# Four plain first groups, an earlier count of ready tiles and an earlier split in a hybrid decoder layer

## The chip, the cores and the metric

The kernel runs on one core of a Trainium2 chip. The metric is the time of one execution on the device in microseconds (us), the median of several runs. Its five engines are named as the profile names them: TensorE is PE (its weight loads PEld), VectorE is DVE, ScalarE is ACT, GpSimd is POOL and SyncE is SP. SP issues nearly all DMAs.

## What is computed

One decoder layer on 256 tokens with a model width of 2048, all in float32, cut to its core:

```python
mod = silu(c) @ w_ada + b_ada
shift1, scale1, gate1, shift2, scale2, gate2 = split(mod, 6)
h = rms_norm(x, g_norm1) * (1 + scale1) + shift1
p = h @ w_in            # 2048 x 12288: retention q,k,v,g | HGRN2 q,f,i,g | gates A, B
y_a = (head_layer_norm(retention(rope(q), rope(k), v)) * silu(g)) @ w_ret_o
y_b = (head_rms_norm(hgrn2(silu(q), f, i)) * silu(g)) @ w_hg_o
x = x + gate1 * ((sigmoid(ga) * y_a + sigmoid(gb) * y_b) @ w_out)
h2 = rms_norm(x, g_norm2) * (1 + scale2) + shift2
a, b = split(causal_conv3(h2 @ w_up))      # 2 x 5632 columns
x = x + gate2 * ((silu(a) * b) @ w_down)
out = rms_norm(x, g_final)
```

Both heads work on chunks of 128 tokens.

## The kernel before

**Products in three parts.** A float32 product is made of three products of a shorter format (fp32r). Weights come by DMA into a buffer `raw` (`load`, L161, at most 11 at a time). ACT copies them into a high part `wh` (`upper`, L176), DVE makes the rest `wl = raw - wh` (`rest`, L181); there are four buffers of each. The activations `hT` have a high and a low part too. A product is high x high, low x high and high x low: L205, L206 and L210 where tokens or columns lie in rows (`mm_rows`), L221, L222 and L225 in the other form (`mm_cols`). `mm_plain` (L231) multiplies the unsplit weights by an unsplit activation as plain float32; its matmuls appear twice each in the profile. `mm_apart` (L242) does the three parts of several groups in turn.

**Pieces and visits.** The first stage makes 12 groups of 512 columns of `w_in` (`ATT`, numbered 0 to 11). The contraction has 16 k tiles of 128. A group can't be done in one go, because the activation tile k exists only after the conditioning for it: `ada1(k)` multiplies 2 MB of `w_ada` by silu(c) on DVE (`ada_dot`, four times L507 for a tile, each with its own `raw`), puts scale and shift together on ACT (L518, L519, L524) and makes the tile on ACT and DVE (`modulated`, L434, L435, L436). So a table of **visits** `(group, m, work)` goes round the groups, and each visit adds m new k tiles to its group; `work` counts units, one k tile of one group. `READY` says at which `work` one more k tile counts as ready. A visit works in **pieces** of two k tiles, or of one where m is odd, each with its own load, split and matmuls. It takes a PSUM bank pair `pg` (there are two), and at its end `take` evicts it: ACT copies it the first time (L880), DVE adds it to the accumulator later (L882). Groups 0 and 1 keep their banks `po` throughout (`RESIDENT = 2`).

Ahead of the table stands a start written by hand for the first four groups (`FIRST = 4`) and k tiles 0 and 1: groups 0 and 1 take tile 0 as plain products, groups 2 and 3 take it as split ones, and then all take tile 1. In this part `pin` keeps instructions in the order of the program; behind it (`self.ordered = False`) the recording layer puts them in an order of its own, so that what the code traces first need not come first on an engine.

**What runs beside it.** `pump`, once for each piece, advances background work by a credit: the conditioning tiles, then the two halves of the HGRN2 head (`hgrn`), retention and the later conditioning vectors. `finish(*ada[:have])` forces the tiles that a visit needs. `early` traces the first piece of the next visit, its load and split, ahead of the present visit's eviction. `hgrn` for a half starts as soon as its three groups are done (0, 2, 4, then 1, 3, 5) and starts on ACT with a sigmoid (L617), which loads a function table; then come Sqrt (L629), Ln (L631) and exponentials, and at its end the head output: matmuls L763 and L765, squares on ACT (L769), a root (L353, with a table load of its own), and products on DVE (L773).

**The wide groups.** Behind the visits four groups of 512 columns are made by `wide_group` (L255 and L258). Each takes both `pg` pairs at once, one for each pair of output blocks, and goes through the k tiles in four steps of four tiles, in each step first one pair and then the other. At its end ACT copies a part (L276) and DVE adds the rest (L277), and only then is the pair free for the next group. The eight gate groups, `w_hg_o`, `w_ret_o`, `w_out`, `w_up` and `w_down` follow.

The two lines on which the table of visits rested:

```python
READY = (14, 24, 34, *range(45, 156, 11))
have = 2 + sum(work >= at for at in READY)
```

Of the kernel before, what the change touches and what calls it, by code (L numbers as in the profile page):

```python
# [12 lines left out]
F32 = mybir.dt.float32  # L13
# [3 lines left out]
AF = mybir.ActivationFunctionType  # L17
ALU = mybir.AluOpType
# [5 lines left out]
KT = D // P  # L24
# [5 lines left out]
G = 512  # L30
NORM_EPS = 1e-6
HEAD_EPS = 1e-5
FIRST = 4
RESIDENT = 2
ADA_EVERY = 11
READY = (14, 24, 34, *range(45, 156, 11))
NOSYNC = mybir.DependencyInfo(mybir.DependencyClass.NoSync, mybir.DependencyReason.DATA)
SMALL = 70
COLS = (8, 8)
# [21 lines left out]
class Kernel:  # L61
# [784 lines left out]
    def run(self):  # L846
        nc, a = self.nc, self.a
# [11 lines left out]
        def act(k):  # L859
            return hT[k // 2][:, k % 2, :]  # L860
# [13 lines left out]
        mms = [self.mm_rows if c0 in ROWS else self.mm_cols for c0 in ATT]  # L874

        def take(g, ps, fresh):
            for at, z in self.parts(ps, ATT[g] in ROWS):
                dst = accs[g][:, at, :]
                if fresh:
                    nc.scalar.activation(dst, z, AF.Copy)  # L880
                else:
                    nc.vector.tensor_tensor(dst, dst, z, ALU.add)  # L882
# [6 lines left out]
        def first(k):  # L889

            return self.scale_shift("ada1", k, s1, t1, self.gn1, fine=True)

        def opening(k):

            z = self.s1([P, T], name="z")
            self.pin(nc.scalar.activation(z, self.xT[0][:, k, :], AF.Identity, bias=self.dots[:, 0:1], scale=s1[:, k : k + 1]))
            return z

        ada = [None, None, *(ada1(k) for k in range(2, KT))]
        gen = first(0)  # L900
# [7 lines left out]
        z = opening(0)  # L908
        for _ in gen:
            pass  # L910
        h = self.s1([P, T], name="h")
        summed(h, z, self.dots)

        ps = {0: self.po2(), 1: self.po2()}
        hT[0] = self.blk([P, 2, 2 * T], F32R, name="hT")
        hi, lo = act(0)[:, :T], act(0)[:, T:]
        plain = [self.load(a["wa"][g][:, 0:1, :], 1, G) for g in range(RESIDENT)]
        uppers = []
        for g in range(RESIDENT, FIRST):
            if g == RESIDENT:  # L920
                self.pin(nc.scalar.activation(hi, h, AF.Copy))
            uppers.append(self.upper(a["wa"][g][:, 0:1, :], 1, G, shift=COLS))
        self.pin(nc.vector.tensor_tensor(lo, h, hi.bitcast(F32), ALU.subtract))
        rests = [self.rest(z) for z in uppers]
        self.times(1, 1, rx_sb)
        gen = first(1)
        for g in range(RESIDENT):
            self.mm_plain(ps[g], plain[g][:, 0, :], h)
        for g in range(RESIDENT, FIRST):
            ps[g] = self.pg()  # L930
            wh, wl = rests[g - RESIDENT]
            mms[g](ps[g], [(act(0), wh[:, 0, :], wl[:, 0, :])], True, False)
            for _ in range(2):
                next(gen)
        z = opening(1)
        for _ in gen:
            pass
        uppers = [self.upper(a["wa"][g][:, 1:2, :], 1, G, shift=COLS) for g in range(RESIDENT)]
        hi, lo = act(1)[:, :T], act(1)[:, T:]
        summed(hi, z, self.dots)  # L940
        h = self.s1([P, T], name="h")
        summed(h, z, self.dots)
        self.pin(nc.vector.tensor_tensor(lo, h, hi.bitcast(F32), ALU.subtract))
        rests = [self.rest(z) for z in uppers]
        self.mm_apart([ps[g] for g in range(RESIDENT)], rests, act(1))
        for g in range(RESIDENT, FIRST):
            wh, wl = self.rest(self.upper(a["wa"][g][:, 1:2, :], 1, G, shift=COLS))
            mms[g](ps[g], [(act(1), wh[:, 0, :], wl[:, 0, :])], False, True)
        begun = list(self.pieces(a["wa"][FIRST][:, 0:2, :], 2))
# [13 lines left out]
        def visit(g):  # L963
            return COLS if g in cols else (0, 0)
# [3 lines left out]
        def begin(kind, hb, *ins):  # L968
            att.append(self.start(kind(hb, *ins, gates)))

        def visits():
            work, g = sum(done), FIRST
            seen = list(done)
            while min(seen) < KT:
                have = 2 + sum(work >= at for at in READY)
                m = have - seen[g]
                if m > 0:
                    yield g, m, work
                    seen[g] = have
                    work += m  # L980
                else:
                    work += 0.5
                g = (g + 1) % len(ATT)
                if have == KT and seen[0] < KT:
                    g = min(i for i in range(len(ATT)) if seen[i] < KT)

        def early(g, m):
            k = done[g]
            pieces = self.pieces(a["wa"][g][:, k : k + m, :], m, shift=visit(g), raw=stock.pop(g, None))
            return chain([next(pieces)], pieces)  # L990

        small = False
        plan = list(visits())
        for g in range(RESIDENT, FIRST):
            take(g, ps[g], True)
        for n, (g, m, work) in enumerate(plan):
            if work > SMALL and not small:
                small = True
                self.small_loads(nc.sync, ("freq", "lbT", "lmask"))
                self.start(self.trig())  # L1000
                self.start(self.lower_bound())
            fresh = done[g] == 0
            have = done[g] + m
            self.finish(*ada[:have])
            bank = ps[g] if g < RESIDENT else self.pg()
            whole = g >= RESIDENT
            self.products(mms[g], bank, a["wa"][g], act, done[g], m, first=whole, last=whole or have == KT, shift=visit(g), begun=begun)
            done[g] = have
            begun = early(*plan[n + 1][:2]) if n + 1 < len(plan) else None
            if whole or have == KT:  # L1010
                take(g, bank, fresh or not whole)
            if have == KT and ATT[g] in GATES:
                nc.scalar.activation(accs[g], accs[g], AF.Silu)
                gates[GATES.index(ATT[g])] = accs[g]
            for hb in range(2):
                gs = [hb, 2 + hb, 4 + hb]
                if g in gs and min(done[i] for i in gs) == KT:
                    self.pace(0, 14.0, 24)
                    begin(self.hgrn, hb, *(accs[i] for i in gs))
                    for i in gs:  # L1020
                        accs[i] = None
# [63 lines left out]
        for j in range(4):  # L1085
            last = j == 3
            x1.append(self.load_rows(j))
            if not last:
                g = self.row(self.gate["gate1"], j, "g1")
            if j == 2:  # L1090
                g3 = self.row(self.gate["gate1"], 3, "g1")
            elif last:
                g = g3
            ps = self.products(self.mm_rows, self.po2() if last else self.pg(), a["wout"][j], actm, 0, KT, hold=4 * last, gain=g if last else None)
            if last:
                g = None
# [14 lines left out]
        begun = [next(up), next(up)]  # L1111
        pu = self.pg()[:2] + self.pg()[:2]

        def half(j, t):

            return self.modulated_half(turned[j], 2 * j, self.sc2, self.sh2, t)
# [6 lines left out]
        for t in range(NT):  # L1123
            self.residual(x1[3], ps, g, None, 3, t)
            if t == 1:
                h = half(0, 0)
# [272 lines left out]
```

## Time and profile before

| | |
|---|---|
| median of 3 runs | 1512.08 us (1510.61 to 1512.22) |
| the profiled execution | 1513.45 us |
| its span | 1511.7 us |
| PE, DVE, ACT busy | 1489.2, 1209.0, 836.8 us |
| HBM read | 382.11 MB, 254 GB/s over the span |

The span reaches from the first to the last instruction of the program that the profiler saw; the execution's own time has some 1.75 us around it. The profile is of one execution. In its rows a time is counted from the start of the span; a row of the timeline has start, duration, engine, line, operation, what is written and read, and in brackets the idle time of the engine before it with what ended it. The page's forty slices show where DMA is full: the first quarter and a bit.

```profile
DMA  9999997788688879989947777777777767667561
```

The first stage with its visits fills the time to about 293 us, the wide groups that to about 398 us.

### The profile page before, as it was taken

What the parts mean: (1) busy time and instruction counts of PE and PEld (TensorE: products, weight loads), DVE (VectorE), ACT (ScalarE), POOL (GpSimd) and SP (SyncE); (2) the same over time, 40 slices, a digit from 0 to 9 for tenths busy, and PEclk for the clock granted to TensorE, in tenths of its full rate; (3) what the DMA queues carried; (4) which work ended last, traced back from release to release, by engine and by line L of the source; (5) the groups of instructions that cost most, each with busy time, mean ns of one, the idle gap of its engine ahead of it and who ended that gap; (6) DMA issues with size and microseconds to landing.
All of it is one profiled execution on the core that took longest, in us unless ns stands there. A gap on an engine that the chain in (4) does not pass through costs nothing.

```text
span 1511.7 us, 22801 instructions
## 1 busy us (share of the span) xinstructions
PE 1489.2 (99%) x8537; PEld 1278.6 (85%) x8537; DVE 1209.0 (80%) x1651; ACT 836.8 (55%) x1207; POOL 4.0 (0%) x8
## 2 busy tenths in 40 slices
PE   9999999998999999999999999999999999999997
PEld 8788898887878888888888888888888888888886
DVE  7799997899899977888877787778777769455694
ACT  5655555866775664445456555555555558344342
POOL 0000000000000000000000000000000000000000
PEclk9999999999999999999999999999999999999999
DMA  9999997788688879989947777777777767667561
GB/s 372 329 337 333 333 332 259 233 287 280 216 268 295 295 259 333 318 292 344 338 133 233 245 228 242 238 233 234 233 243 230 228 195 201 197 206 213 179 188 56
DMA packets 111311, 385.73 MB, mean 255 GB/s; under 512 B 12848, under 2 KB 13408, under 8 KB 111200
## 3 DMA queue, kind: packets, MB, share of 16 engines
q1 hardware_dynamic: 110304, 383.14, 76.8%
q8 instruction: 67, 1.10, 0.3%
q10 hardware_dynamic: 896, 1.13, 0.2%
q14 instruction: 44, 0.36, 0.1%
HBM read 382.11 MB, written 2.11 MB: 254 GB/s over the span
## 4 chain that ended last, share of the span: by engine, by line
PE 93%; DVE 3%; ACT 1%; DMA 1%; issue 1%; DVEq 0%; ACTq 0%
PE pg L205 13%; PE pg L210 13%; PE pg L206 13%; PE po L1232 11%; PE pg L1232 10%; PE po L1234 5%; PE pg L1234 5%; PE pg L255 4%; PE po L210 3%; PE po L205 3%; PE po L206 3%; PE pg L258 2%; DVE raw L507 1%; DVE wl L181 1%; DMA raw<-in_wa 1%
## 5 line engine op out<-in xcount | busy, mean ns | idle before, releaser
L181 DVE TENSOR_TENSOR wl<-raw,wh 128x1024 fp32r<-128x1024 f32 (+1 forms) x534 | 633.5, 1194 | 229.5 <-ACT wh L176 215.1
L176 ACT ACTIVATE wh<-raw 128x1024 fp32r<-128x1024 f32 (+1 forms) x534 | 546.1, 1034 | 471.0 <-PE pg L206 192.2
L507 DVE SCALAR_TENSOR_TENSOR raw<-raw,sc 128x1024 f32<-128x1024 f32 (+2 forms) x194 | 234.4, 1212 | 0.0
L205 PE MATMUL pg<-wh,hT 128*128 128x512 f32 x512 | 203.3, 397 | 4.3 <-ACT wh L176 3.0
L206 PE MATMUL pg<-wh,hT 128*128 128x512 f32 x512 | 200.1, 391 | 0.0
L1232 PE MATMUL po<-h2T,wh 128*128 128x512 f32 x704 | 175.8, 392 | 0.0
L1232 PE MATMUL pg<-h2T,wh 128*128 128x512 f32 x688 | 172.2, 393 | 0.0
L1232 PEld LDWEIGHTS po<-h2T,wh 128*128 128x128 f32 x704 | 125.8, 188 | 21.6
L1232 PEld LDWEIGHTS pg<-h2T,wh 128*128 128x128 f32 x688 | 123.0, 188 | 21.1
L210 PE MATMUL pg<-wl,hT 128*128 128x512 f32 x512 | 139.3, 392 | 0.0
L205 PEld LDWEIGHTS pg<-wh,hT 128*128 128x128 f32 x512 | 96.5, 188 | 25.7 <-ACT wh L176 3.7
L210 PEld LDWEIGHTS pg<-wl,hT 128*128 128x128 f32 x512 | 96.7, 189 | 20.5
L206 PEld LDWEIGHTS pg<-wh,hT 128*128 128x128 f32 x512 | 96.5, 189 | 19.3
L1234 PEld LDWEIGHTS po<-h2T,wl 128*128 128x128 f32 x704 | 93.4, 188 | 7.5
L1234 PEld LDWEIGHTS pg<-h2T,wl 128*128 128x128 f32 x688 | 91.4, 188 | 7.3
L1234 PE MATMUL po<-h2T,wl 128*128 128x256 f32 x704 | 94.6, 277 | 0.0
L1234 PE MATMUL pg<-h2T,wl 128*128 128x256 f32 x688 | 92.5, 277 | 0.0
L255 PE MATMUL pg<-hT,wh 128*128 128x512 f32 x256 | 66.0, 401 | 4.7 <-DVE p L277 4.7
L206 PE MATMUL pg<-wh,gs 128*128 128x512 f32 x176 | 68.6, 390 | 0.0
L205 PE MATMUL pg<-wh,gs 128*128 128x512 f32 x176 | 68.6, 390 | 0.0
L205 PE MATMUL po<-wh,gs 128*128 128x512 f32 x176 | 68.6, 390 | 0.0
L206 PE MATMUL po<-wh,gs 128*128 128x512 f32 x176 | 68.5, 389 | 0.0
(271 smaller groups left out, 2021.1 us busy)
## 6 DMA issues: line engine op xcount, KB each, us to landing
raw<-in_wup SPq DMA_DIRECT2D x176, 512.0 KB, 4.6
raw<-in_wdown SPq DMA_DIRECT2D x88, 512.0 KB, 4.1
raw<-in_wa SPq DMA_DIRECT2D x80, 512.0 KB, 5.4
raw<-in_ada SPq DMA_DIRECT2D x64, 512.0 KB, 5.5
raw<-in_wab SPq DMA_DIRECT2D x64, 512.0 KB, 5.4
raw<-in_ada SPq DMA_DIRECT2D x62, 512.5 KB, 5.6
raw<-in_gate SPq DMA_DIRECT2D x32, 512.5 KB, 5.2
raw<-in_wk SPq DMA_DIRECT2D x32, 512.0 KB, 4.6
```

The source lines that it names most:

```text
L176: self.pin(self.nc.scalar.activation(wh, raw, AF.Copy))
L181: self.last = self.nc.vector.tensor_tensor(wl, raw, wh.bitcast(F32), ALU.subtract)
L205: nc.tensor.matmul(ps[t], lhsT=act[:, hi], rhs=wh, start=first and i == 0, stop=False)
L206: nc.tensor.matmul(ps[t], lhsT=act[:, lo], rhs=wh, start=False, stop=False)
L210: nc.tensor.matmul(ps[t], lhsT=act[:, hi], rhs=wl, start=False, stop=last and i == len(items) - 1)
L255: nc.tensor.matmul(ps[z], lhsT=wh[:, z * P : (z + 1) * P], rhs=act, start=first and i == 0, stop=False)
L258: nc.tensor.matmul(ps[z][:, :T], lhsT=wl[:, z * P : (z + 1) * P], rhs=act[:, :T], start=False, stop=last and i == len(items) - 1)
L507: dot = self.pin(nc.vector.scalar_tensor_tensor(raw[:, 0, :], raw[:, 0, :], 1.0, self.sc[:, at:to], ALU.mult, ALU.mult, accum_out=part[:, ...
L1232: self.pin(nc.tensor.matmul(ps[z], lhsT=wh[:, z * P : (z + 1) * P], rhs=act, start=kt == 0, stop=False, skip_group_check=bool(begun)))
L1234: nc.tensor.matmul(ps[z][:, :T], lhsT=wl[:, z * P : (z + 1) * P], rhs=act[:, :T], start=False, stop=kt == KT - 1, skip_group_check=bool(be ...
```

## The change

The diff, whole but for its context:

```diff
-READY = (14, 24, 34, *range(45, 156, 11))
+LAG = 1
...
-        plain = [self.load(a["wa"][g][:, 0:1, :], 1, G) for g in range(RESIDENT)]
-        uppers = []
-        for g in range(RESIDENT, FIRST):
-            if g == RESIDENT:
-                self.pin(nc.scalar.activation(hi, h, AF.Copy))
-            uppers.append(self.upper(a["wa"][g][:, 0:1, :], 1, G, shift=COLS))
-        self.pin(nc.vector.tensor_tensor(lo, h, hi.bitcast(F32), ALU.subtract))
-        rests = [self.rest(z) for z in uppers]
+        plain = [self.load(a["wa"][g][:, 0:1, :], 1, G) for g in range(FIRST)]
         self.times(1, 1, rx_sb)
         gen = first(1)
-        for g in range(RESIDENT):
+        for g in range(FIRST):
+            if g >= RESIDENT:
+                ps[g] = self.pg()
             self.mm_plain(ps[g], plain[g][:, 0, :], h)
-        for g in range(RESIDENT, FIRST):
-            ps[g] = self.pg()
-            wh, wl = rests[g - RESIDENT]
-            mms[g](ps[g], [(act(0), wh[:, 0, :], wl[:, 0, :])], True, False)
-            for _ in range(2):
+            if g == 1:
+                self.pin(nc.scalar.activation(hi, h, AF.Copy))
                 next(gen)
+                next(gen)
+                self.pin(nc.vector.tensor_tensor(lo, h, hi.bitcast(F32), ALU.subtract))
+        next(gen)
+        next(gen)
...
-                have = 2 + sum(work >= at for at in READY)
+                have = min(KT, 2 + int((work - LAG) / ADA_EVERY))
...
         plan = list(visits())
+        z = [n for n, (g, _, _) in enumerate(plan) if g == FIRST + 2]
+        for n, m in zip(z, (-1, 1)):
+            plan[n] = (plan[n][0], plan[n][1] + m, plan[n][2])
...
+            ahead = early(*plan[n + 1][:2]) if m <= 2 and n + 1 < len(plan) else None
             self.products(mms[g], bank, a["wa"][g], act, done[g], m, first=whole, last=whole or have == KT, shift=visit(g), begun=begun)
             done[g] = have
-            begun = early(*plan[n + 1][:2]) if n + 1 < len(plan) else None
+            begun = ahead or (early(*plan[n + 1][:2]) if n + 1 < len(plan) else None)
```

It has four parts. All four first groups take k tile 0 as plain products, so the two splits of weights for it go, and the low part of the activation is made later. The table of ready tiles becomes a formula: tile 3 counts as ready at 23 units rather than 24, and the visits fall otherwise on the groups. Group 6 takes one tile less in its first visit and one more in its second. And the next visit's first piece is traced ahead of the products wherever the present visit has at most two tiles. The table has 53 visits instead of 54; its last ones were (group, tiles) (3,3) (4,3) (5,2) (6,2) (7,1) (8,1) (9,1) (11,5) and are (3,3) (4,2) (5,2) (6,1) (7,1) (8,1) (10,5) (11,4). Tile 3 is first wanted in visit 10 (the tenth from 0, group 10, second piece) instead of visit 11; tiles 4 and 5 one unit sooner than before; tiles 6 to 15 after as many units as before.

How this moves instructions is shown at three places. The first is the start, on DVE, from the scale and shift of tile 0 (L887 writes `h`) to the dots for tile 1 (L507). Before:

```order
L887 TENSOR_SCALAR h_224<-z_216,dot_39_210 128x256
L923 TENSOR_TENSOR hT_230<-h_224,hT_230 128x256
L181 TENSOR_TENSOR wl_239<-raw_236,wh_238 128x512
L181 TENSOR_TENSOR wl_244<-raw_241,wh_243 128x512
L497 TENSOR_TENSOR xT_113<-xT_113,rx_sb 128x256
L507 SCALAR_TENSOR_TENSOR raw_272,dot_57_271<-raw_272,sc 128x1024
L507 SCALAR_TENSOR_TENSOR raw_275,dot_57_271<-raw_275,sc 128x1025
```

And of the changed kernel:

```order
L887 TENSOR_SCALAR h_224<-z_216,dot_39_210 128x256
L497 TENSOR_TENSOR xT_113<-xT_113,rx_sb 128x256
L507 SCALAR_TENSOR_TENSOR raw_250,dot_54_249<-raw_250,sc 128x1024
L507 SCALAR_TENSOR_TENSOR raw_253,dot_54_249<-raw_253,sc 128x1025
L928 TENSOR_TENSOR hT_230<-h_224,hT_230 128x256
L507 SCALAR_TENSOR_TENSOR raw_270,dot_59_269<-raw_270,sc 128x1024
```

The two `wl` are gone, and the low part (L923, now L928) stands behind two dots.

The second place is the end of the visits, on DVE: the adds of groups 5 to 8 (`p_174` to `p_177`) among the splits of the next pieces. Before, with the scans of the HGRN2 head (L636) among them:

```order
L882 TENSOR_TENSOR p_174<-p_174,pg_2760 128x1024
L181 TENSOR_TENSOR wl_2834<-raw_2831,wh_2833 128x512
L636 SCALAR_TENSOR_TENSOR b_2775<-ones,f_2773 128x128 x3
L882 TENSOR_TENSOR p_175<-p_175,pg_2784 128x1024
L181 TENSOR_TENSOR wl_2849<-raw_2846,wh_2848 128x1024
L882 TENSOR_TENSOR p_176<-p_176,pg_2807 128x1024
L882 TENSOR_TENSOR p_177<-p_177,pg_2822 128x1024
```

And of the changed kernel:

```order
L882 TENSOR_TENSOR p_174<-p_174,pg_2711 128x1024
L181 TENSOR_TENSOR wl_2771<-raw_2768,wh_2770 128x1024
L882 TENSOR_TENSOR p_175<-p_175,pg_2735 128x1024
L882 TENSOR_TENSOR p_176<-p_176,pg_2752 128x1024
L181 TENSOR_TENSOR wl_2800<-raw_2797,wh_2799 128x1024
L882 TENSOR_TENSOR p_177<-p_177,pg_2767 128x1024
L636 SCALAR_TENSOR_TENSOR b_2732<-ones,f_2730 128x128 x3
```

The scans have moved behind the add of group 8, and one split stands between the adds of groups 5 and 6.

The third place is the border of the third and fourth wide group, on ACT, from the first squares of the head output to the evictions L276 of the third group (`pg_3508` and `pg_3509` before, `pg_3517` and `pg_3518` now). Before:

```order
L769 ACTIVATE sqh_3781,ssh_3780<-po_3775 128x128
L176 ACTIVATE wh_3902<-raw_3900 128x1024
L353 ACT_TABLE_LOAD
L353 ACTIVATE rsh_3786<-ssh_3780,eps_73 128x4
L769 ACTIVATE sqh_3819,ssh_3818<-po_3809 128x128 x3
L531 ACTIVATE gate_2933<-dot_567_3890 128x1
L769 ACTIVATE sqh_3819,ssh_3818<-po_3809 128x128
L276 ACTIVATE p_3831<-pg_3508 128x512
L353 ACTIVATE rsh_3824<-ssh_3818,eps_73 128x4
L276 ACTIVATE p_3831<-pg_3509 128x512
L617 ACT_TABLE_LOAD
L617 ACTIVATE f_3869<-p_170 128x1024
```

And of the changed kernel:

```order
L769 ACTIVATE sqh_3697,ssh_3696<-po_3691 128x128
L176 ACTIVATE wh_3818<-raw_3816 128x1024
L353 ACT_TABLE_LOAD
L353 ACTIVATE rsh_3702<-ssh_3696,eps_73 128x4
L769 ACTIVATE sqh_3738,ssh_3737<-po_3728 128x128 x4
L531 ACTIVATE gate_2903<-dot_549_3779 128x1
L353 ACTIVATE rsh_3743<-ssh_3737,eps_73 128x4
L617 ACT_TABLE_LOAD
L617 ACTIVATE f_3783<-p_170 128x1024
L276 ACTIVATE p_3803<-pg_3517 128x512
L622 ACTIVATE f_3783<-f_3783,lb,lb_1685 128x256
L276 ACTIVATE p_3803<-pg_3518 128x512
```

The second root and the start of the second half of the head (L617) have moved ahead of both evictions. On PE the matmuls that feed these squares move against the group's own, from the first of them to the group's end. Before, with the fourth group's first row last:

```order
L763 MATMUL po_3775<-p_173,at_3115 128x128 x4
L255 MATMUL pg_3509<-hT_1978,wh_3743 128x512 x4
L255 MATMUL pg_3509<-hT_2290,wh_3749 128x512 x4
...
L763 MATMUL po_3809<-p_173,at_3115 128x128
L765 MATMUL po_3809<-p_173,a_481_3167 128x128
L255 MATMUL pg_3836<-hT_230,wh_3840 128x512 x4
```

And of the changed kernel:

```order
L763 MATMUL po_3691<-p_173,at_3018 128x128 x4
L255 MATMUL pg_3518<-hT_1335,wh_3664 128x512 x4
L255 MATMUL pg_3518<-hT_1662,wh_3670 128x512 x4
...
L763 MATMUL po_3728<-p_173,at_3018 128x128
L765 MATMUL po_3728<-p_173,a_468_3081 128x128
L255 MATMUL pg_3517<-hT_1930,wh_3752 128x512 x4
...
L255 MATMUL pg_3518<-hT_1930,wh_3752 128x512 x4
...
L255 MATMUL pg_3808<-hT_230,wh_3812 128x512 x4
```

The head output stands two pairs of output blocks earlier: before, one pair followed its first matmuls and then the fourth group began; now the pair that followed is that of the third step, and both pairs of the fourth step come behind the head output.

## The prediction

> **What bounds the kernel now.** First the page: TensorE (PE) is busy nearly all the time.
>
> ```profile
> span 1511.7 us, 22801 instructions
> PE 1489.2 (99%) x8537; PEld 1278.6 (85%) x8537; DVE 1209.0 (80%) x1651; ACT 836.8 (55%) x1207; POOL 4.0 (0%) x8
> ```
>
> So a change can win only where PE waits: 1511.7 - 1489.2 = 22.5 us, part of it the end of the program, which the change leaves alone. The view of PE's waits says where (line, what ended the wait, total, times, longest):
>
> ```profile
> PE pg L255 <- DVE p L277: 4.7, 1, 4.7
> PE pg L205 <- ACT wh L176: 3.0, 2, 2.1
> PE po L242 <- DVE hT L887: 1.4, 1, 1.4
> PE po L221 <- ACT wh L176: 1.1, 1, 1.1
> PE pg L205 <- DVE p L882: 1.1, 2, 0.6
> ```
>
> All of these lie in the first 375 us, and the change moves nothing behind the gates but a step or so of the background work. Then the windows, for the room that the other engines have (columns: window; busy us of PE, weight load, DVE, ACT, POOL; granted clock; DMA share; GB/s):
>
> ```profile
> 90.00:105.00 15.00, 15.00 (x68) 12.44 (x67) 15.00 (x21) 5.79 (x10) 0.00 (x0) 1.00 0.97 328
> 400.00:500.00 100.00, 100.00 (x805) 82.36 (x804) 97.46 (x139) 65.11 (x101) 0.00 (x0) 1.00 0.82 281
> ```
>
> From 90 to 105 us three resources are full at once: PE, DVE and DMA. What is won for PE alone ahead of there may be lost there again; what takes work off DVE counts.
>
> **Term 1, the border of the third and fourth wide group: -5.5.** It is the longest wait, so it comes first. PE's rows, then ACT's:
>
> ```profile
> 361.19 1.99 PE L255 MATMUL pg<-hT,wh 128*128 128x512 f32 x8
> 363.02 1.10 PE L258 MATMUL pg<-hT,wl 128*128 128x256 f32 x8
> 363.95 1.05 PE L763 MATMUL po<-p,at 128*128 128x128 f32 x8
> ...
> 369.18 0.39 PE L765 MATMUL po<-p,a 128*128 128x128 f32 x2
> 374.31 3.25 PE L255 MATMUL pg<-hT,wh 128*128 128x512 f32 x8 [4.74 <-DVE p L277]
> ```
>
> ```profile
> 365.04 0.28 ACT L769 ACTIVATE sqh<-po 128x128 f32<-128x128 f32 x1 [3.47 <-PE po L763]
> ...
> 366.51 0.30 ACT L531 ACTIVATE gate<-dot 128x1 f32<-128x1 f32 x1 [1.10 <-DVE raw L507]
> ...
> 372.60 0.59 ACT L276 ACTIVATE p<-pg 128x512 f32<-128x512 f32 x1
> ...
> 373.88 1.28 ACT L617 ACT_TABLE_LOAD   x1
> ```
>
> The fourth group's first bank is that of the third. Its eviction L276 stood on ACT behind the squares, the table load and the roots of the head output, which began 365.04 - 363.95 = 1.1 after the first L763 and held ACT for 372.60 - 365.04 = 7.56. PE had one more pair of output blocks and the second head product left, was through with them at 369.4, and waited.
>
> In the changed order L763 stands two pairs earlier on PE, but on ACT L276 has moved behind one more root, a table load (1.3 by the row) and a sigmoid (as long as a split of its size, 0.95): 2.5 with the root. So L276 starts 1.1 + 7.56 + 2.5 = 11.2 after L763, and PE may go 374.31 - 372.60 = 1.7 later at most, 1.3 where DVE is free for L277: 12.5. PE by then has done what it did from 363.95 to 369.4, 5.45, and two pairs of 363.95 - 361.19 = 2.76: 11.0. That leaves a wait of 1.5; without the 1.10 that ACT stood for a dot it is 0.4. I take 0.9. Before, the wait was 4.74, and behind it the granted clock (the third number from the right) was halved, as once before:
>
> ```profile
> 43.80:47.20 3.40, 3.40 (x10) 2.63 (x9) 3.40 (x6) 1.08 (x2) 0.00 (x0) 0.50 0.96 325
> 374.90:378.30 3.40, 3.40 (x12) 2.83 (x11) 0.89 (x3) 3.36 (x6) 0.95 (x1) 0.50 0.44 177
> ```
>
> 3.4 us at half speed cost 1.7. The waits of 1.4 and 1.1 had no such follower, so 0.9 is too short for it. 4.74 + 1.7 - 0.9 = 5.5; from 4.9 to 6.4.
>
> **Term 2, the start: -1.1.**
>
> ```profile
> 18.54 3.72 PE L231 MATMUL po<-h,raw 128*128 128x256 f32 x16 [0.43 <-DVE h L887]
> 21.91 0.47 PE L221 MATMUL pg<-hT,wh 128*128 128x256 f32 x1
> ...
> 26.45 2.10 PE L242 MATMUL po<-hT,wh 128*128 128x256 f32 x16 [1.41 <-DVE hT L887]
> ```
>
> ```profile
> 18.07 0.41 DVE L887 TENSOR_SCALAR h<-z,dot 128x256 f32<-128x256 f32 x1
> ...
> 20.71 0.42 DVE L497 TENSOR_TENSOR xT<-xT,rx_sb 128x256 f32<-128x256 f32 x1
> 21.04 1.22 DVE L507 SCALAR_TENSOR_TENSOR raw<-raw,sc 128x1024 f32<-128x1024 f32 x1
> ...
> 25.90 0.41 DVE L887 TENSOR_SCALAR hT<-z,dot 128x256 fp32r<-128x256 f32 x1
> ```
>
> Two plain groups hold PE for 21.91 - 18.54 = 3.37, so four end at 18.54 + 6.74 = 25.3. On DVE the activation's low part moves behind two dots and two `wl` go: L497 starts at 18.5 instead of 20.7, the dots (21.04 to 25.90, 4.86) run from 18.85, and with 0.35 for the low part the second activation comes at about 24.1, if the weights of the dots have landed by then, which I take. PE is then the later one: L242 starts at 25.3, 1.1 sooner. Bounds: 0 (late landings) to 1.15. Two raw buffers are now let go by PE, some 3 us later than by DVE before; SP's issues behind them slip, but DMA has a queue of landings there, so I put that at 0, at most 1.
>
> The next wait stays. PE's longest one of the first round ended at 42.48, and ACT shows why:
>
> ```profile
> 40.46 1.02 ACT L880 ACTIVATE p<-pg 128x1024 f32<-128x1024 f32 x1 [0.28 <-PE pg L210]
> 41.38 1.05 ACT L176 ACTIVATE wh<-raw 128x1024 fp32r<-128x1024 f32 x1
> ```
>
> The split of the next weights stands behind an eviction that waits for PE. `ahead` traces that split before the products, but on ACT the changed kernel still has the eviction of group 6 right ahead of it. So the 2.1 us stay, and I keep the halved clock of 43.8 to 47.2 behind them in the sum, 1.7. [...]
>
> **Term 3, an activation tile wanted sooner: +0.5.** A tile's six matmuls take 6 x (363.02 - 361.19) / 8 = 1.37. Tile 3 was wanted after 28 units (k tile times group), now after 25: 4.1 us sooner. ACT's durations for it:
>
> ```profile
> 58.14 0.28 ACT L524 ACTIVATE t<-dot 128x1 f32<-128x1 f32 x1
> 58.46 0.60 ACT L434 ACTIVATE hT<-xT,t,s 128x256 fp32r<-128x256 f32 x1
> ```
>
> In the changed order an eviction (41.38 - 40.46 = 0.92), L524 (0.32 until the next), two activations (0.60 each, 1.05 together as they overlap) and a split (0.95) stand in a row between the end of visit 9 and the second piece of visit 10: 3.2 us, against a first piece of 2.74. That makes 0.5; from 0 to 2.2, if the last dots come late too.
>
> **Term 4, one eviction fewer on a full DVE: -1.0,** and **term 5, the short visits: -0.4.** Both rest on the add-evictions, two here:
>
> ```profile
> 284.00 2.35 DVE L882 TENSOR_TENSOR p<-p,pg 128x1024 f32<-128x1024 f32 x2
> ```
>
> After the full DVE of 90 to 105 us PE waits for tile 6. It is wanted after 58 units in both kernels; 17 visits end ahead of it before, now 16, so DVE has one add fewer to do, 1.15. I take 1.0, from 0 to 1.2.
> At the end three one-tile visits of 1.37 us follow each other over two banks, each with an add and a `wl` on DVE, and PE waits twice for L882, 1.1 in all. In the changed order, counted from the end of group 5: its add until 1.15, a `wl` of 1024 columns until 2.3, the add of group 6 until 3.45. Group 8 wants that bank at 2.74, so some 0.7 is left, and the next bank is free in time: 0.4 won; from 0 to 1.1.
>
> What follows is late by nothing that I see: from 400 to 500 DVE is busy for 97%, but PE waited for it nowhere, and the scans of the second half now stand ahead of the last border, where DVE had room.
>
> **Sum.** -5.5 - 1.1 + 0.5 - 1.0 - 0.4 = -7.5. The profiled execution took 1513.45 (its span 1511.7, 1.75 around it): 1505.95. It lies 1.4 above the median of the runs, 1512.08; I carry half of that over: **1505.3**.
>
> **Rivals.**
> - The early gains are lost. Between 60 and 130 us DVE and DMA set the pace, so terms 2, 4 and 5 go for nothing and the border stays at 4.9: 1513.45 - 4.9 = 1508.5, or with term 3 at its 2.2, 1510.75. For it: the full DVE and DMA. Against it: DVE has less to do now.
> [...]
> - The change doesn't do at the border what the order says: the squares wait for something else than L763, as the 1.10 for a gate's dot was, but for 4 us. Then 4.74 and 1.7 stay: 1513.45 - 2.0 = 1511.4.
> - Slower: at the first border of the wide groups the second eviction now stands behind a copy, two exponentials and two splits, 5 us after the first. I count 0.7 of room there. If DVE, and ACT behind it, runs 3 us late, PE waits 2.3 + 1.7 there, and at the third border the chain is 2.5 longer than before: 1513.45 - 2.0 + 4.0 + 2.5 = 1518. It decides from a lag of some 3 us on; against it speaks that PE waited at none of the other borders.
>
> **Chances.** Forecast (1502.8 to 1508) 0.55; early gains lost (1508 to 1511) 0.20; more (below 1502.8) 0.13; nothing at the border 0.07; slower 0.05. 0.2%, about what a measurement of this kernel can tell from no change, is 3.0: faster is below 1509.1, slower above 1515.1. Faster: 0.55 + 0.13 + two fifths of 0.20 = 0.76; same 0.12 + 0.07 = 0.19; slower 0.05. The range from 1501 to 1510.5 leaves out some 0.06 below and 0.14 above.
>
> **What would show it.** L242 starts near 25.3 without a wait; a wait of 2 us ahead of visit 7, at about 41.4; half a us in visit 10; the wait for tile 6 shorter by one; one wait for an add-eviction at the end, not two; no halved clock between 360 and 380, and a wait under 1.5 at the third border. Wrong would be a wait for L277 over 2 us, a new wait at another border, or waits for DVE behind 400 us.

## The result, and the profile after

| | before | changed |
|---|---|---|
| median of 5 runs in the comparison | 1512.22 us (1510.61 to 1513.54) | 1504.68 us (1503.57 to 1504.91) |
| ratio, 95% interval | | 0.9948 (0.9934 to 0.9963) |
| the profiled execution, its span | 1513.45, 1511.7 us | 1504.62, 1502.8 us |

The changed kernel is 7.5 us faster, 0.5%, by the medians, and 8.9 us by the two spans. The page of the changed kernel has the same bound, with 2.3 us of PE's time and 6.6 us of its waiting gone:

```profile
span 1502.8 us, 22779 instructions
PE 1486.9 (99%) x8529; PEld 1274.8 (85%) x8529; DVE 1206.8 (80%) x1647; ACT 834.9 (56%) x1204; POOL 4.0 (0%) x8
```

The view of PE's waits (engine, line, what ended the wait: total, times, longest) shows where. The 4.7 us for L277 have become 0.3, one of the two waits for L882 is gone, and so is the 1.1 of L221; the 2.1 for a split is still the longest.

```profile
PE pg L205 <- ACT wh L176: 2.7, 2, 2.1
PE po L242 <- ACT wh L176: 1.2, 1, 1.2
...
PE pg L205 <- DVE p L882: 0.6, 1, 0.6
...
PE pg L255 <- DVE p L277: 0.3, 1, 0.3
PE po L225 <- DVE wl L181: 0.2, 1, 0.2
```

**The border of the third and fourth wide group.** The timeline of PE, and then of ACT, in the changed kernel:

```profile
355.38 1.05 PE L763 MATMUL po<-p,at 128*128 128x128 f32 x8
...
360.76 2.09 PE L255 MATMUL pg<-hT,wh 128*128 128x512 f32 x8
...
366.86 2.11 PE L255 MATMUL pg<-hT,wh 128*128 128x512 f32 x8 [0.32 <-DVE p L277]
```

```profile
356.47 0.28 ACT L769 ACTIVATE sqh<-po 128x128 f32<-128x128 f32 x1 [1.65 <-PE po L763]
...
363.25 1.28 ACT L617 ACT_TABLE_LOAD   x1
364.54 1.06 ACT L617 ACTIVATE f<-p 128x1024 f32<-128x1024 f32 x1
365.51 0.58 ACT L276 ACTIVATE p<-pg 128x512 f32<-128x512 f32 x1
```

L276 starts 365.51 - 355.38 = 10.1 us after the first L763, and PE goes on 1.35 later, at 366.86. In the meantime it had the head output and three pairs of output blocks to do (the last two, from 360.76 and 363.62, are the fourth step), two more than before, so it waited 0.32 only. The windows of the clock (third number from the right) show what went with it, before and after:

```profile
360.00:380.00 20.00, 15.26 (x88) 13.48 (x87) 15.23 (x27) 14.88 (x35) 1.90 (x2) 0.91 0.80 300
```

```profile
360.00:380.00 20.00, 19.68 (x115) 17.16 (x115) 16.27 (x32) 19.80 (x32) 1.91 (x2) 1.00 0.82 298
```

**The start.** PE and DVE in the changed kernel:

```profile
17.06 3.72 PE L231 MATMUL po<-h,raw 128*128 128x256 f32 x16 [0.42 <-DVE h L887]
20.61 3.62 PE L231 MATMUL pg<-h,raw 128*128 128x256 f32 x16
25.39 1.87 PE L242 MATMUL po<-hT,wh 128*128 128x256 f32 x14 [1.16 <-ACT wh L176]
```

```profile
18.90 1.23 DVE L507 SCALAR_TENSOR_TENSOR raw<-raw,sc 128x1024 f32<-128x1024 f32 x1 [1.56 <-DMA raw<-in_ada]
...
20.78 1.23 DVE L507 SCALAR_TENSOR_TENSOR raw<-raw,sc 128x1025 f32<-128x1025 f32 x1 [0.65 <-DMA raw<-in_ada]
...
24.83 0.41 DVE L887 TENSOR_SCALAR hT<-z,dot 128x256 fp32r<-128x256 f32 x1
```

L242 starts at 25.39, but with a wait of 1.16, since in this execution PE began 1.5 us sooner (17.06 instead of 18.54) and DVE stood 1.56 and 0.65 us for the weights of the dots. The split L176 that ended PE's wait stands on ACT behind work on these dots.

**The first round of visits.** ACT and PE again:

```profile
39.41 1.03 ACT L880 ACTIVATE p<-pg 128x1024 f32<-128x1024 f32 x1 [0.30 <-PE pg L210]
40.33 1.05 ACT L176 ACTIVATE wh<-raw 128x1024 fp32r<-128x1024 f32 x1
```

```profile
41.43 0.50 PE L205 MATMUL pg<-wh,hT 128*128 128x512 f32 x1 [2.06 <-ACT wh L176]
...
58.98 0.50 PE L205 MATMUL pg<-wh,hT 128*128 128x512 f32 x1 [0.65 <-ACT wh L176]
```

```profile
42.50:45.90 3.40, 3.40 (x10) 2.63 (x9) 3.40 (x7) 1.33 (x2) 0.00 (x0) 0.50 1.04 411
```

The split of group 7's first weights stands behind the eviction of group 6, PE waits 2.06, and the clock is halved behind it, as before. The 0.65 at 58.98 is new: k tile 3, now wanted in group 10's visit.

**Three stretches.** For the experiments the program is cut at the first L242 (the end of the start) and at the first wide group, whose first row was, before and now:

```profile
293.60 0.62 PE L255 MATMUL pg<-hT,wh 128*128 128x512 f32 x2
```

```profile
290.57 2.00 PE L255 MATMUL pg<-hT,wh 128*128 128x512 f32 x8
```

The visits took 293.60 - 26.45 = 267.15 before and 290.57 - 25.39 = 265.18 now, 2.0 less; from there to the end of the span it was 1511.7 - 293.60 = 1218.1 and is 1502.8 - 290.57 = 1212.2, 5.9 less; the start is 1.1 shorter in these two executions.

### The profile page after: what moved, and what is told of

The parts are those of the page before. It is cut to its first block, busy times and chain, and to the rows that moved or that the text cites. A ratio compares the mean times of both kernels' runs of the same rounds, so it can differ in the third digit from the quotient of the medians.

```text
span 1502.8 us, 22779 instructions
## 1 busy us (share of the span) xinstructions
PE 1486.9 (99%) x8529; PEld 1274.8 (85%) x8529; DVE 1206.8 (80%) x1647; ACT 834.9 (56%) x1204; POOL 4.0 (0%) x8
## 4 chain that ended last, share of the span: by engine, by line
PE 95%; DMA 2%; DVE 2%; ACT 1%; issue 0%; DVEq 0%; SPq 0%; ACTq 0%
PE pg L205 14%; PE pg L210 14%; PE pg L206 13%; PE po L1232 11%; PE pg L1232 11%; PE po L1234 5%; PE pg L1234 5%; PE pg L255 4%; PE po L210 3%; PE po L205 3%; PE po L206 3%; PE pg L258 2%; DMA raw<-in_ada 1%; PE pg L221 1%; PE pg L222 1%; PE pg L225 1%
## 5 line engine op out<-in xcount | busy, mean ns | idle before, releaser
L176 ACT ACTIVATE wh<-raw 128x1024 fp32r<-128x1024 f32 (+1 forms) x531 | 544.1, 1037 | 463.6 <-PE pg L206 192.1
L507 DVE SCALAR_TENSOR_TENSOR raw<-raw,sc 128x1024 f32<-128x1024 f32 (+2 forms) x194 | 234.1, 1210 | 2.2 <-DMA raw<-in_ada 2.2
L205 PE MATMUL pg<-wh,hT 128*128 128x512 f32 x512 | 203.0, 396 | 3.4 <-ACT wh L176 2.7
L206 PE MATMUL pg<-wh,hT 128*128 128x512 f32 x512 | 200.2, 391 | 0.0
L205 PEld LDWEIGHTS pg<-wh,hT 128*128 128x128 f32 x512 | 96.4, 188 | 24.9 <-ACT wh L176 3.8
L206 PEld LDWEIGHTS pg<-wh,hT 128*128 128x128 f32 x512 | 96.4, 188 | 19.3
L206 PE MATMUL pg<-wh,gs 128*128 128x512 f32 x176 | 68.6, 390 | 0.0
L205 PE MATMUL pg<-wh,gs 128*128 128x512 f32 x176 | 68.5, 389 | 0.0
L205 PE MATMUL po<-wh,gs 128*128 128x512 f32 x176 | 68.5, 389 | 0.0
L206 PE MATMUL po<-wh,gs 128*128 128x512 f32 x176 | 68.5, 389 | 0.0
L1245 ACT ACTIVATE u<-uy,convw 128x256 f32<-128x256 f32 x88 | 52.3, 595 | 28.7 <-DVE uy L1243 28.4
```

The lines of the kernel that those rows point to most:

```text
L176: self.pin(self.nc.scalar.activation(wh, raw, AF.Copy))
L205: nc.tensor.matmul(ps[t], lhsT=act[:, hi], rhs=wh, start=first and i == 0, stop=False)
L206: nc.tensor.matmul(ps[t], lhsT=act[:, lo], rhs=wh, start=False, stop=False)
L507: dot = self.pin(nc.vector.scalar_tensor_tensor(raw[:, 0, :], raw[:, 0, :], 1.0, self.sc[:, at:to], ALU.mult, ALU.mult, accum_out=part[:, ...
L1245: nc.scalar.activation(u, y, AF.Identity, bias=w[3], scale=w[2])
```

## The experiments

All were timed beside the kernel before, five runs of each and eleven of e1_plain and e4_border_back; the median of the kernel before was 1512.37, 1512.33 and 1512.52 us in the three sessions (the first four, the next four, the last two rows). The last three columns are of the profiled execution.

| run | what it is | median us | ratio, 95% interval | first L242 | visits | rest |
|---|---|---|---|---|---|---|
| e1_plain | before + four plain groups | 1513.31 | 1.0003 (0.9994 to 1.0013) | 25.46 | 267.2 | 1218.1 |
| e2_count | before + formula | 1503.53 | 0.9944 (0.9931 to 0.9956) | 25.89 | 263.6 | 1212.4 |
| e3_border_now | before + credit 3.3 | 1506.72 | 0.9963 (0.9951 to 0.9976) | 25.32 | 267.1 | 1212.4 |
| e4_border_back | changed, credit -3.3 | 1511.33 | 0.9993 (0.9984 to 1.0002) | 26.69 | 265.3 | 1218.7 |
| e5_noshift | changed, no shift in group 6 | 1502.84 | 0.9937 (0.9923 to 0.9951) | 26.31 | 262.7 | 1212.4 |
| e6_oldstart | changed, old start | 1505.30 | 0.9951 (0.9937 to 0.9965) | 26.90 | 265.1 | 1212.3 |
| e7_split | changed, split ahead of eviction | 1502.65 | 0.9937 (0.9924 to 0.9950) | 25.36 | 262.9 | 1212.4 |
| e8_again | the changed kernel | 1504.99 | 0.9952 (0.9939 to 0.9965) | 25.27 | 265.2 | 1212.4 |
| e9_shift10 | e7 + shift in group 10 | 1501.63 | 0.9927 (0.9914 to 0.9939) | 25.30 | 261.9 | 1212.4 |
| e10_addback | changed, one visit cut in two | 1505.75 | 0.9951 (0.9937 to 0.9964) | 25.61 | 266.2 | 1212.5 |

The last two columns repeat to 0.3 us wherever the visits and the border are the same, except for e4_border_back's rest (0.6 more, with a halved clock of some 6.8 us at the border, 0.51 on the mean from 371 to 378 us, where the kernel before has 3.4). The first L242 does not.

### Single parts: the start, and the formula

The first is the kernel before with the start of the changed kernel, the second the kernel before with the formula:

```diff
-        plain = [self.load(a["wa"][g][:, 0:1, :], 1, G) for g in range(RESIDENT)]
...
+        plain = [self.load(a["wa"][g][:, 0:1, :], 1, G) for g in range(FIRST)]
```

```diff
-                have = 2 + sum(work >= at for at in READY)
+                have = min(KT, 2 + int((work - LAG) / ADA_EVERY))
```

> The kernel before with the first part of the change alone: all four first groups take k tile 0 as plain products, the low part of the activation behind two dots. By the prediction's second term: the first L242 starts near 25.3 us, all that PE waits for behind it stays as it was (2.1 us near 41.4 with the halved clock behind it, 4.7 us for L277 at the border of the third and fourth wide group): 1.1 us less than before, near 1511. Rival, the early gains are lost on the full DVE and DMA: the wide groups begin when they began before and the time is that of before. A second thing to read: the first L231 started at 18.54 us before and at 17.06 us in the changed kernel, with the same instructions ahead of it; if this is chance, it will be spread over that range in these runs, whatever the kernel.

> The kernel before with the formula for the ready tiles alone (53 visits), without the plain groups, the shift in group 6 and the split traced ahead. Theory: the number of visits, by the count of background steps that it pumps, is what moves the head output two pairs of output blocks to the front, so the wait for L277 goes to 0.3 to 1.5 us and the halved clock behind it with it: 5.5 us less, and the adds and the short visits give up to 1.4 us more, while group 6 now wants k tile 2 in its first visit, one unit sooner, which costs up to 1.4 us: 1505 to 1507.5. Rival, the border needs the other parts too: the wait of 4.7 us stays and the time is 1510.5 to 1512.

The four plain groups alone gave nothing in the median: their interval reaches from 0.9 us less to 2.0 more, just short of the 1.1 forecast. All waits behind the start are those of before, the visits take 267.2 us as they did, so nothing was given back later. The first L231 lay anywhere from 17.06 to 19.97 us in the profiles of this study, with the same instructions ahead of it. That spread is larger than the term, so only executions that began alike can be compared. DVE wrote the first activation `h` (L887) at 17.00 in the profile of e1_plain, and at 16.95 in that of e3_border_now, which has the old start. The first L242 of e1_plain, and then of e3_border_now:

```profile
25.46 2.11 PE L242 MATMUL po<-hT,wh 128*128 128x256 f32 x16
```

```profile
25.32 2.10 PE L242 MATMUL po<-hT,wh 128*128 128x256 f32 x16 [1.41 <-ACT wh L176]
```

After such a beginning the old start is as early as the new one; e2_count, with the old start too, has 25.89 for an `h` at 16.79. The 26.45 of the kernel before belongs to an `h` at 18.07, and e5_noshift, with four plain groups and an `h` at 18.08, has 26.31. At 18.53 and 18.54 it is 26.90 with the old start (e6_oldstart) and 26.69 with the new one (e4_border_back). By such pairs the four plain groups win between nothing and 0.5 us.

The formula alone gave 8.8 us by the medians, more than the whole change (the intervals of the two overlap; the run without the shift, below, tells them apart). The rest is 5.7 shorter, the border's share, so it needs no other part. But the visits are 3.5 us shorter, against 2.0 with all parts. PE's rows and the clock near 41 us show why:

```profile
40.30 0.50 PE L205 MATMUL pg<-wh,hT 128*128 128x512 f32 x1 [0.45 <-ACT hT L434]
41.58 0.50 PE L206 MATMUL pg<-wh,hT 128*128 128x512 f32 x1 [0.78 <-DVE hT L436]
```

```profile
40.00:48.00 8.00, 6.92 (x29) 5.53 (x30) 7.45 (x12) 5.58 (x8) 0.00 (x0) 1.00 1.03 409
```

With three tiles in group 6's first visit PE has a third tile to start on while group 7's weights are split: two waits of 0.45 and 0.78 replace the one of 2.06, and the clock stays full.

### The border alone, there and back

One line, in the kernel before with 3.3 and in the changed kernel with -3.3:

```diff
         self.pace(0, 143.0, 88)
+        self.credit[0] = 3.3
```

> The kernel before with one line more: the background work of the wide groups begins with a credit of 3.3 instead of 0, so the first head output stands on PE and ACT as in the changed kernel; the table of visits and the start are untouched. Theory: the wait for L277 at the third border falls from 4.7 to under 1.5 us, no halved clock between 360 and 380 us, 5.5 us less than before: near 1506.6. Rival, the gain of the changed kernel comes from the visits (fewer evictions, an earlier start), and the border is only where it shows: less than 2 us, 1510 or more.

> The changed kernel with one line more: the background work of the wide groups begins 3.3 us in debt, so the first head output stands on PE and ACT as in the kernel before. Theory: the wait of 4.7 us for L277 and the halved clock behind it are back, 5.5 us more than the changed kernel: near 1510.2, and what is left of the gain, some 2 us, is that of the visits and the start. Rival: the order at the border isn't what decides, the time stays near 1504.7.

The first row is PE's at the border in the kernel before with a credit of 3.3, the second in the changed kernel with the debt:

```profile
368.73 2.10 PE L255 MATMUL pg<-hT,wh 128*128 128x512 f32 x8 [0.32 <-DVE p L277]
```

```profile
372.67 3.75 PE L255 MATMUL pg<-hT,wh 128*128 128x512 f32 x8 [4.76 <-DVE p L277]
```

The place of the head output alone gave 1512.37 - 1506.72 = 5.7 us on the kernel before, and taking it away cost the changed kernel 1511.33 - 1504.99 (e8_again) = 6.3. The visits kept their length both times. So the border is the larger part of the gain, and it is a matter of how far the background work has got, whatever brought it there. e2_count's expectation put it down to the number of visits; that is wrong, since e10_addback has 54 visits and its rest is still 1212.5. In the table of visits 14 tiles follow when groups 0, 2 and 4 are done and the first half of the head begins, where 12 followed before: so the background gets more credit ahead of the wide groups; this is read from the table and was not tried by itself.

### Leaving one part out, and the wait near 41 us

```diff
-        z = [n for n, (g, _, _) in enumerate(plan) if g == FIRST + 2]
-        for n, m in zip(z, (-1, 1)):
-            plan[n] = (plan[n][0], plan[n][1] + m, plan[n][2])
```

> The changed kernel without its third part: group 6 takes three tiles in its first visit again and its second visit one less. With the formula alone PE waited near 41 us only 0.45 and 0.78 us, one after the other, and the clock was not halved there; with the shift it waits 2.06 at once and loses 1.7 more to the halved clock. Theory: it is the shift that makes this wait; without it there are two short waits, no halved clock between 40 and 48 us, and from the first L242 to the first wide group 263.6 us as with the formula alone (265.2 in the changed kernel): 1.6 us less than the changed kernel, near 1503.1. Rival, the four plain groups or the split traced ahead make it: the wait of 2.06 and the halved clock stay, 1504.7.

The third part of the change costs 1504.99 - 1502.84 = 2.2 us: without it the visits take 262.7 us, and PE's waits near 41 us are 0.5 and 0.8. The theory held, with 0.6 us more than expected.

This run and e2_count also answer the prediction's fourth term, that one add-eviction fewer on DVE takes away the wait for k tile 6. The longer of that wait's two parts in the kernel before, and with the formula alone:

```profile
107.39 0.50 PE L205 MATMUL pg<-wh,hT 128*128 128x512 f32 x1 [0.94 <-ACT wh L176]
```

```profile
105.15 0.50 PE L205 MATMUL pg<-wh,hT 128*128 128x512 f32 x1 [0.95 <-ACT wh L176]
```

By the table e2_count and e5_noshift have 16 visits ahead of tile 6, as the changed kernel has, and still they wait as before, 0.25 and then 0.95 us in both. The wait is gone in the changed kernel and in e7_split (below), which have the shift in group 6. On DVE three adds stand among the four dots of tile 6 in the kernel before, in e2_count and in e5_noshift, and two in the changed kernel and in e7_split. So it was the shift that took this wait away, and not the number of visits; how the shift moves the add wasn't looked into.

The next run takes the changed kernel with the start of before:

```diff
+        uppers = []
+        for g in range(RESIDENT, FIRST):
+            if g == RESIDENT:
+                self.pin(nc.scalar.activation(hi, h, AF.Copy))
+            uppers.append(self.upper(a["wa"][g][:, 0:1, :], 1, G, shift=COLS))
```

> The changed kernel without its first part: groups 2 and 3 take k tile 0 as split products again. Two values for the start are open. By the prediction's second term the four plain groups are worth 1.1 us, so 1505.8. By the run of that part alone they are worth nothing in the median (ratio 1.0003, from 0.9994 to 1.0013), so 1504.7. In the profile: from the first L231 to the first L242 7.8 to 7.9 us, as in the three kernels with the old start, and from there to the wide groups as long as in the changed kernel (265.2).

1505.30 against 1504.99: by the medians the four plain groups are worth 0.3 us, less than the spread of these runs, 1503.65 to 1506.31. The expected 7.8 us from L231 to L242 did not come, it was 6.98: in that execution PE began late (19.92), and the second activation was already on its way. The fourth part wasn't run by itself: in the changed kernel the rows of PE, ACT, DVE and SP stand in the same order without it.

In the seventh run one dependence puts group 6's eviction behind group 7's first split:

```diff
                 if fresh:
-                    nc.scalar.activation(dst, z, AF.Copy)
+                    ins = nc.scalar.activation(dst, z, AF.Copy)
+                    if g == FIRST + 2:
+                        self.tc.add_manual_dep(ins.ins, self.high.ins.name, NOSYNC, reason="behind the split of the next piece")
```

> The changed kernel with one dependence more: on ACT the eviction of group 6 goes behind the first split of group 7, where it stood ahead of it and held it until PE was done with group 6. Theory: the split then starts when its weights have landed and the high part's sibling is made, at about 39.7 us instead of 40.33, so PE waits 1.4 us instead of 2.06. That is 0.6 us less, 1504.1; and as a wait of 1.41 us at the start had no halved clock behind it while 2.06 had one, the halved clock may go too: 1502.4. Rival, the weights land later than that, or the eviction is then late for the next bank: 1504.7 or more.

> The changed kernel once more, to stand beside the other three on the same chip: 1504.7, and from the first L242 to the first wide group 265.2 us. The start is read again: with a halved clock between 13 and 20 us in some executions, the first L231 near 18.4 and L242 near 25.4; without it, L231 near 17.1 and L242 at the same 25.4, since the second activation waits for the weights of the dots to land.

ACT's split starts at 39.62, the eviction behind it, and PE (its lines are one higher in this kernel: L206 was L205) waits 1.39; the windows from 40 to 48 us have the full clock:

```profile
39.62 1.04 ACT L176 ACTIVATE wh<-raw 128x1024 fp32r<-128x1024 f32 x1
40.56 1.01 ACT L881 ACTIVATE p<-pg 128x1024 f32<-128x1024 f32 x1
```

```profile
40.71 0.50 PE L206 MATMUL pg<-wh,hT 128*128 128x512 f32 x1 [1.39 <-ACT wh L176]
```

```profile
40.00:48.00 8.00, 7.29 (x32) 6.01 (x33) 6.28 (x9) 6.33 (x10) 0.00 (x0) 1.00 1.03 405
```

1504.99 - 1502.65 = 2.3 us: 0.7 of wait, and 1.7 that the halved clock had cost (3.4 us at 0.50). With its shift this kernel is as fast as e5_noshift without (1502.84), so what cost time was the wait, not the shift as such.

### One wait further, and one eviction put back

```diff
-        z = [n for n, (g, _, _) in enumerate(plan) if g == FIRST + 2]
-        for n, m in zip(z, (-1, 1)):
-            plan[n] = (plan[n][0], plan[n][1] + m, plan[n][2])
+        for f in (FIRST + 2, FIRST + 6):
+            z = [n for n, (g, _, _) in enumerate(plan) if g == f]
+            for n, m in zip(z, (-1, 1)):
+                plan[n] = (plan[n][0], plan[n][1] + m, plan[n][2])
```

> The run e7_split (1502.65) with the shift made for group 10 as well: one tile less in its first visit, one more in its second, so k tile 3 is first wanted by group 11, three tiles of products later (4.1 us). The wait of 0.66 us in group 10's first visit (0.81 lost) should go, and nothing new come in its place in group 11's. What then remains open is whether PE, 0.8 us sooner, waits that much longer for k tile 6 near 90 us, where DVE is full (0.24 lost there now). Kept: 1501.9. Given back: 1502.6. The order at the borders of the wide groups is that of the changed kernel, 1204.2 us from the first wide group to the last matmul.

1.0 us less than e7_split by the medians of two sessions and by the visits of the two profiles, and the fastest kernel of the study: 1501.63 us, 0.9927 of the kernel before, and 3.4 us under e8_again. The wait of 0.65 in group 10's visit is gone, but two new ones came for it, 0.48 at 68.87 and 0.21 at 100.89. So the gain isn't that wait; smaller delays that e7_split has at 89, 125 and 128 us are gone too, and what removed them wasn't tried.

```diff
+        n = z[1] - 1
+        g, m, work = plan[n]
+        plan[n : n + 1] = [(g, 2, work), (g, m - 2, work + 2)]
```

> The changed kernel with one visit cut in two: group 5's second visit of four tiles becomes two of two, so the table has 54 visits as before and DVE one add-eviction of 1.15 us more ahead of k tile 6. Two questions. The prediction's fourth term: if the evictions on the full DVE set when tile 6 is there, PE loses 0.9 to 1.2 us more near 91 us (1.1 to 1.4 instead of 0.24) and the time is 1505.9; if not, the loss stays at 0.24 and the time at 1504.9. And the border: if the number of visits as such decides where the first head output stands, the wait of 4.7 us is back (1511); if it is the tiles that follow when groups 0, 2, 4 are done (14 now, 12 before), it is not.

In this kernel the second of the two halves multiplies the weights of the first again. The visits take 1.1 us longer than e8_again's, about one add-eviction. But PE did not lose it at k tile 6 (which is wanted after 100 us; the 0.24 near 91 us, which the expectation took for it, is a wait for a `wl`). It lost it 30 us later, at a split. PE's row, and ACT's ahead of that split:

```profile
136.53 0.39 PE L221 MATMUL pg<-hT,wh 128*128 128x256 f32 x1 [1.22 <-ACT wh L176]
```

```profile
134.11 0.30 ACT L524 ACTIVATE t<-dot 128x1 f32<-128x1 f32 x1 [4.17 <-DVE raw L507]
```

The split stands on ACT behind L524, which waited for a dot on DVE; in e8_again L524 came at 132.37. So in this kernel DVE carried its arrears on, and they came out where a later visit was short of something.

## Why the prediction was right, point by point

- **The bound and the border (-5.5).** Right in place, mechanism and size: 5.9 us less from the first wide group to the end by the two profiles, 5.7 by e3_border_now. L276 came 10.1 us after L763 where 11.2 was worked out: the wait for a gate's dot (1.10 before) did not fall into this stretch, which is the lower of the two ends that the prediction gave (0.4 of wait, 0.32 measured). The halved clock went too (1.00 from 360 to 380 us).
- **The start (-1.1).** L242 came at 25.39 where 25.3 was forecast, but not for the reason given, so this agreement is luck. The step that failed is "if the weights of the dots have landed by then, which I take". They hadn't: DVE waited 1.56 and 0.65 us for them in the changed kernel's profile. L242 stood at 25.4 to 25.6 whether PE began at 17.06, at 18.21 (e7_split), at 18.31 (e10_addback) or at 18.37 (e1_plain); from 18.55 on it is the four plain groups that set it, 6.7 to 6.9 us behind the first L231. The 1.1 between the two profiles is mostly that of two executions that began apart: after an early beginning the old start has 25.32 as well (e3_border_now). The term is 0.3 us by e6_oldstart and none by e1_plain.
- **The wait near 41 us.** It stayed, with its halved clock (0.50 from 42.50 to 45.90 us), as forecast. That it was the change's own third part that kept it was not seen: the sum took it as given, and with the formula alone it would have gone.
- **k tile 3 (+0.5).** 0.65 measured, in the visit named.
- **One eviction fewer (-1.0) and the short visits (-0.4).** The wait for tile 6 is gone as forecast, but not for the reason given: with the same 16 visits ahead of it e2_count and e5_noshift wait as before, and e10_addback, with 17, doesn't wait. The wait went with the shift in group 6, so that the fourth term's size was luck. Of the two waits for L882 one is gone, as forecast (0.6 for 1.1). Mis-sized was what follows: the 1.1 us that PE had waited for a split at 128 us went as well, and 0.4 at 75 us, so the visits won 2.0 where the sum of the three terms was 0.9. An eviction put back (e10_addback) costs 1.1 us, which is the length of an add, at another place.
- **The sum.** Forecast -7.5 against the profile's own time, measured -8.8 (1513.45 to 1504.62); against the medians, 1505.3 forecast and 1504.68 measured. The start's missing gain and the visits' larger one made up for each other, which is luck; the border, the largest term, was right by itself.
- **The rivals.** "The early gains are lost" holds for the start in the main, not for the visits, and not by the mechanism given: the start's gain never came, and nothing was lost between 60 and 130 us. The wait of 3 us at another border didn't come: the others show none.

By parts, then, in medians: the formula is worth 8.8 us, the shift in group 6 takes 2.2 back, the four plain groups are worth 0.3, inside the spread of the runs, and the split traced ahead changes no order.

## What to carry to other kernels

A change of several parts can be right in its sum and hold a part that costs; run each alone, above all where a wait that "stays" could have gone. Look for what stands ahead of an eviction or a split in the queue of a lightly used engine: here 5.7 us hung on how early the head output began, whose chain on ACT an eviction stands behind, and 2.3 on the order of one split and one eviction on ACT, which was busy for 56% of the time. Before a chain is called shorter, see when its data lands, and compare executions that began alike.

## What the runs showed of the hardware

**The length of a wait and the clock.** In seven profiles with the wait of 2.06 us near 41 us (before, changed, e1, e4, e6, e8, e10) some 3.4 us at half clock followed (0.50 from 42.50 to 45.90 us in the changed kernel); behind the waits of 1.39 us (e7_split, e9_shift10) and of 0.45 and 0.78 (e2_count; 0.5 and 0.8 in e5_noshift) none did, and the clock was 1.00 from 40.8 to 47.6 us. The halved stretch began between 0.0 us (e8_again, e10_addback) and 1.3 us (before) behind the end of the wait. In e8_again the clock changed at 14.12, 17.54, 41.43 and 44.84, which is 3.42, 23.89 and 3.41 us apart. What a wait between 1.39 and 2.06 us does near 41 us, no run shows.

**A halved clock at the start, in most profiles.** In nine of the twelve profiles (not in before, changed and e3_border_now) the clock was halved between 12 and 20 us, for some 3.4 us in seven of them and some 6.8 in e4_border_back and e6_oldstart. The 18 filler matmuls (L248) ahead of the first L231 took 2.17 us in the changed kernel's first profile and 3.09 in that of e8_again, the same program, where it was:

```profile
14.46 2.17 PE L248 MATMUL pg<-ones 128*128 128x128 f32 x18
```

```profile
15.62 3.09 PE L248 MATMUL pg<-ones 128*128 128x128 f32 x18
```

```profile
13.60:17.00 3.40, 3.40 (x19) 3.32 (x19) 3.16 (x9) 1.62 (x5) 0.00 (x0) 0.58 1.06 405
```

The fillers then end behind the activation that they were to bridge: at 15.62 + 3.09 = 18.71 by their row in e8_again, where L887 ends at 17.62 + 0.41 = 18.03. In the changed kernel's first profile L231 started 0.47 us behind the start of L887 (17.06 and 16.59), in e8_again 0.93 (18.55 and 17.62): the halved clock cost L231 some 0.5 us, and the other 1.0 by which it was later came from DVE. Neither reached L242, which started at 25.39 and 25.27, and the two executions took 1504.62 and 1504.60 us.
